# Tiles that TensorE streams, laid out with their even columns first and read in turns

## The chip, the cores and the metric

The kernel runs on one core of a Trainium2 chip. The metric is the device time of one execution, in microseconds (us). TensorE is called PE in the profile's rows (PEld is its weight load), VectorE DVE, ScalarE ACT, GpSimd POOL and SyncE SP.

## The reference

Two layers over a stream `x` of 1024 positions and 1024 channels, in float32. The first layer is a gated multi-scale causal pooling mixer, the second a gated sliding-window attention (window 128, 16 heads, 2 shared key/value heads) with sinks and a relative-position bias. Cut to what matters:

```
h = modulate(rmsnorm(x, norm_g[0]), shift, scale)          # layer 0
u, z = split(h @ a_w_in, 2)
p = trailing means of u over 2, 4, 8, 16 positions, minus u
y = (grouped(p @ a_w_group) * a_scale * silu(z)) @ a_w_out
x = x + gate * y
k, v = split(modulate(rmsnorm(x, kv_norm_g), ...) @ w_kv)  # shared by the heads
h = modulate(rmsnorm(x, norm_g[1]), shift, scale)          # layer 1
q, z = split(h @ b_w_in, 2)
per block of 128 queries, with this and the previous block of 128 keys:
    s = q k / 8 + pos_bias, masked to the band
    o = softmax(s with one sink per head) v
y = (o * silu(z)) @ b_w_out
x = x + gate * y
return rmsnorm(x, final_g)
```

## The kernel before, in words

Channels lie on the 128 partitions and positions along the free dimension, so that a tile of activations is 128 channels by 512 positions (`H = 512`, half of the sequence, index `q`). Every product of two float32 matrices is made from three matmuls: each operand is split into a high part (rounded to the 4-byte type fp32r) and a low part (what is left), and high times high, high times low and low times high are added up in one PSUM bank. The stationary operand is a 128x128 piece of a weight, the moving operand ("what TensorE streams") is the 128x512 tile of activations.

So each tile of activations is written twice. ScalarE writes the high part (`nc.scalar.copy` or `nc.scalar.activation` with an fp32r output), and VectorE the low part (a subtraction of the high part from the source). GpSimd does this in one place (`split_wg`). These pairs stand in `split_wg`, `first_h` and `first_l`, `pool_split`, `block_sums`, `split_g`, `Modulated.fold_h` and `fold_l`, `keys`, `attend` (the transposed probabilities `ph`, and the heads' outputs that go back into `qt`) and `Second.step`. The matmuls that stream these tiles are in `join_mm` (L308), `first_mm` (L375), `product` (L648), `passes` (L213), `dense_mm` (L200 to L202), `dense_step` (L1222 to L1224), `scores` in `attend` (L1358 and L1359, whose moving operands are the keys `KH` and `KL`) and `blend` (L1422 and L1423, which stream `ph` and its masked copy `pp`). Transposes (L1392, L1557), the sums of squares (L161, L1703), the spreading of a row (L173, L1720) and the last 128 positions' output product (L1580 to L1582, where the weights are the moving operand) stream other tiles.

The order on each engine is fixed when the program is built. Up to the keys and values it is the order of the code (on VectorE and ScalarE partly that of the tile framework). From there on (the attention, about 600 us into the span to its end) a small planner sets it: `note` records each step with its engine and an assumed length, `in_order` keeps TensorE's steps in the order in which they were recorded and places those of the other engines by these lengths. VectorE is where most of its choices fall: preparing the second half's activations (`xn`, then `hm`, in `Second.step`), the softmax rows, the splits and the residual adds share its queue.

Of the kernel before, what the change touches and what calls it, by code (L numbers as in the profile page):

```python
# [12 lines left out]
F32 = mybir.dt.float32  # L13
# [5 lines left out]
P = 128  # L19
# [36 lines left out]
SLOT_FILL = 32  # L56


@with_exitstack
def trunk(ctx, tc, xT, c, pack, ada_first, ada_rest, wu0_in, wg0_in, wa, wg, wao, wkv,  # L60
# [156 lines left out]
    with ExitStack() as sa:  # L217
# [74 lines left out]
        def split_wg(ci):  # L292
            nc.scalar.copy(out=wgs[0][:, ci, :], in_=wgr[:, ci, :])
            nc.gpsimd.tensor_sub(out=wgs[1][:, ci, :], in0=wgr[:, ci, :],
                                 in1=wgs[0][:, ci, :].bitcast(F32))
# [9 lines left out]
        def join_mm(m, ps, ci, passes=(0, 1, 2)):  # L305
            for s in passes:
                a, b = ((0, 0), (0, 1), (1, 0))[s]
                mm(ps, wus[ci][:, a, m * P:(m + 1) * P], wgs[b][:, ci, :],  # L308
                   start=ci == 0 and s == 0, stop=ci == 3 and s == 2)
# [42 lines left out]
        def first_h(k, q):  # L352
# [4 lines left out]
            nc.scalar.activation(h, first_f(k, q), AF.Identity, bias=b, scale=1.0)  # L357

        def first_l(k, q):
            _, b, h, l = first_parts(k, q)  # L360
            nc.vector.scalar_tensor_tensor(out=l, in0=first_f(k, q), scalar=b,
                                           in1=h.bitcast(F32), op0=ALU.add, op1=ALU.subtract)
# [3 lines left out]
        def first_mm(k, q, passes=(0, 1, 2)):  # L366
# [6 lines left out]
            for s, i in order:  # L373
                w, hl = ((0, 0), (1, 0), (0, 1))[s]
                mm(psu[i, q], w0[k // 2][:, k % 2, w, i * P:(i + 1) * P], block(k, q)[hl],  # L375
# [189 lines left out]
        def pool_split(g, ct, u):  # L565
            cur = pooled(g, u)
            p = pts[ct] = xp.tile([P, 2, T], F32R, tag="x", name="p", bufs=4)
            nc.scalar.copy(out=p[:, 0, :], in_=cur)
            nc.vector.tensor_sub(out=p[:, 1, :], in0=cur, in1=p[:, 0, :].bitcast(F32))
# [7 lines left out]
        def block_sums(j):  # L577
# [13 lines left out]
            for i, s, a, shift, b, op0, op1 in parts:  # L591
# [5 lines left out]
                nc.scalar.copy(out=sum_part(i, j, 0), in_=s)  # L597
            for i, s, *_ in parts:
                nc.vector.tensor_sub(out=sum_part(i, j, 1), in0=s,
                                     in1=sum_part(i, j, 0).bitcast(F32))  # L600
# [50 lines left out]
        def pair_products(ws, evac):  # L651

            b_acts = lambda q, c: lambda k, hl: block(4 * c + k, q)[hl]
            s_acts = lambda i: lambda k, hl: sum_part(i, k, hl)
# [49 lines left out]
        z_acts = lambda k, hl, q: block(k, q)[hl]  # L704
# [87 lines left out]
        def split_g(k, raws):  # L792
# [7 lines left out]
            for q in range(2):  # L800
                t = slot("gh") if q == 1 and k >= 14 else g_units[q][:, k % 2]
                g_parts[k, q] = t[:, 0, :], t[:, 1, :]
                nc.scalar.copy(out=t[:, 0, :], in_=raws[q])
                nc.vector.tensor_sub(out=t[:, 1, :], in0=raws[q], in1=t[:, 0, :].bitcast(F32))
# [19 lines left out]
        with tc.manual_schedule(engines={ET.PE}):  # L824
            nxt = w_first
            for i, (kind, g, j) in enumerate(steps):
# [19 lines left out]
                else:  # L846
                    for t in range(2):

                        ps = gemm_full(w, t * 512, lambda k, hl, q: pts[k][:, hl, half(q)],
# [11 lines left out]
            def g_acts(hf):  # L861
                return lambda k, hl, q: g_parts[8 * hf + k, q][hl]
# [84 lines left out]
        def last_chunk(i):  # L947

            n, c = late[i // 4], i % 4
            if c == 0:  # L950
                got[n] = bank(("S", "d")[i // 4 % 2])
            passes([(1, got[n])], ws[n, c // 2], (c % 2) * 512,
                   lambda k, hl, q: g_parts[4 * c + k, q][hl], 4, c == 0, c == 3)


        class Modulated:
# [6 lines left out]
            def fold_h(self, k, f):  # L963
# [7 lines left out]
                nc.scalar.activation(h, f, AF.Identity, bias=b, scale=1.0)  # L971

            def fold_l(self, k):
                _, b, h = self.args(k)
                nc.vector.scalar_tensor_tensor(
                    out=self.tiles[k // 2][:, k % 2, 1, :], in0=self.xn.pop(k), scalar=b,
                    in1=h.bitcast(F32), op0=ALU.add, op1=ALU.subtract)
# [5 lines left out]
            def __call__(self, k, i, q=0):  # L983
                return self.tiles[k // 2][:, k % 2, i, :]
# [231 lines left out]
    def dense_step(ps, w, off, acts, k, n, cols):  # L1216
# [8 lines left out]
        note(PE, {512: 0.69, 384: 0.53}[cols], f,  # L1225
# [9 lines left out]
    def keys(q, hk, ps=None):  # L1235
        def done(ps):
            cols = half(q)
            for kv in range(2):
                a, b = slice(kv * 64, kv * 64 + 64), slice((1 - kv) * 64, (1 - kv) * 64 + 64)

                def high(kv, a, to, h):
                    note(ACT, 0.55, lambda: nc.scalar.copy(out=KH[kv][to, cols], in_=ps()[a, :]),
                         [(ps, 0)], [(KHb[kv], (h, q))])

                def low(kv, a, to, h):
                    note(DVE, 0.63, lambda: nc.vector.tensor_sub(
                        out=KL[kv][to, cols], in0=ps()[a, :], in1=KH[kv][a, cols].bitcast(F32)),
# [84 lines left out]
    def attend(q, r, b):  # L1332
# [15 lines left out]
        def scores(j):  # L1348
# [6 lines left out]
            def f():  # L1355
                for e in range(2):
                    lhs = qt()[:, j, e, cols]
                    mm(s()[:, e, lo:], lhs, KH[kv][:, ks], start=True, stop=False)  # L1358
                    mm(s()[:, e, lo:], lhs, KL[kv][:, ks], start=False, stop=True)  # L1359
            note(PE, 0.48 if b else 0.46, f,  # L1360
# [28 lines left out]
        def turn():  # L1389
# [6 lines left out]
        note(ACT, 0.55, lambda: nc.scalar.copy(out=cur()[:, 0], in_=tp()), [(tp, 0)], [(cur, 0)])  # L1396
        note(DVE, 0.63, lambda: nc.vector.tensor_sub(  # L1397
            out=cur()[:, 1], in0=tp(), in1=cur()[:, 0].bitcast(F32)),
            [(tp, 0), (cur, 0)], [(cur, 1)])
        parts = [(b, cur)]  # L1400
        if b:
            prev = tile_of("pp", bp, [P, 2, H], F32R, 1)
            v8 = lambda t: t.rearrange("p x (a i) -> p (x a) i", i=P)
            note(POOL, 1.12, lambda: nc.gpsimd.affine_select(  # L1404
                out=v8(prev()), in_=v8(cur()).bitcast(F32), pattern=[[0, 8], [-1, P]], base=-1,
# [3 lines left out]
                out=v8(cur()), in_=v8(cur()).bitcast(F32), pattern=[[0, 8], [1, P]], base=0,  # L1409
# [9 lines left out]
        def blend(x, blk, ph):  # L1419
            def f():  # L1420
                v = VS[:, 2 * blk + kv].rearrange("p x c -> p (x c)")
                mm(o(), v, ph()[:, 0], start=x == 0, stop=False)  # L1422
                mm(o(), v, ph()[:, 1], start=False, stop=x == len(parts) - 1)  # L1423
            note(PE, 0.46, f, [(VSb, (blk // 4, 0)), (VSb, (blk // 4, 1)), (ph, 0)]
# [14 lines left out]
        for e in range(2):  # L1439
# [5 lines left out]
        note(ACT, 0.36, lambda: nc.scalar.copy(out=qt()[:, :, 0, cols], in_=ofv()),  # L1445
             [(of, 0), (of, 1)], o_on(0))
        note(DVE, 0.56, lambda: nc.vector.tensor_sub(
            out=qt()[:, :, 1, cols], in0=ofv(), in1=qt()[:, :, 0, cols].bitcast(F32)),
# [3 lines left out]
    def heads(q, part, cs):  # L1452

        def acts(k, i):
# [3 lines left out]
                       lambda t: t[:, k % 2, i, cols])  # L1458
# [321 lines left out]
    class Second:  # L1780
# [5 lines left out]
        def step(self, k):  # L1786
            if k % 2 == 0:
# [7 lines left out]
            note(ACT, 0.66, lambda: nc.scalar.activation(  # L1795
                t()[:, k % 2, 0, :], f(), AF.Identity, bias=b, scale=1.0),
                [(f, 0)], [(t, (k % 2, 0))])
            note(DVE, 0.7, lambda: nc.vector.scalar_tensor_tensor(
                out=t()[:, k % 2, 1, :], in0=f(), scalar=b,
                in1=t()[:, k % 2, 0, :].bitcast(F32), op0=ALU.add, op1=ALU.subtract),  # L1800
                [(f, 0), (t, (k % 2, 0))], [(t, (k % 2, 1))])

        def __call__(self, k, i):
            return Ref(self.tiles[k // 2], ((k % 2, i),), lambda t: t[:, k % 2, i, :])
# [161 lines left out]
```

## Time and profile before

| what | value |
|---|---|
| median of 3 runs | 964.12 us (963.63 to 964.23) |
| span of the profiled execution | 961.6 us |
| TensorE, matmul | 951.3 us (99%), 4468 matmuls |
| TensorE, weight load | 795.6 us (83%) |
| VectorE | 756.2 us (79%) |
| ScalarE | 425.4 us (44%) |
| GpSimd | 143.1 us (15%) |

For the profiled execution the page gives its span, from the first instruction to the last; no time of its own stands beside it. The span is 2.5 us under the median of the runs. Matmuls overlap one another in the records (one lasts about 390 ns and the next starts 227 ns after it), so that TensorE's busy share tells only that it hardly ever pauses; how fast it goes is read from the distance between starts.

### The profile page before, as it was taken

To read this page: it belongs to the slowest core of one execution; us is meant where nothing else is said; L and a number is where in the kernel's file an instruction comes from. 1 tells how busy PE (TensorE), PEld (TensorE's weight loads), DVE (VectorE), ACT (ScalarE), POOL (GpSimd) and SP (SyncE) were. 2 spreads that over 40 slices of the span, in tenths; PEclk is the share of its full clock that TensorE was granted. 3 is DMA by queue.
4 is the path that set the end of the run, shared out by engine and by line. 5 is a ranking of instruction groups with operands and counts; after the bars stand their busy time and mean duration, and the time that the engine had idled before them with its cause. 6 is when DMAs were issued, how large, how long until landed. Compare 5 with 4: busy or idle time off the path is not lost.

```text
span 961.6 us, 12687 instructions
## 1 busy us (share of the span) xinstructions
PE 951.3 (99%) x4468; PEld 795.6 (83%) x4468; DVE 756.2 (79%) x1414; ACT 425.4 (44%) x872; POOL 143.1 (15%) x229
## 2 busy tenths in 40 slices
PE   9999999999999999999999999999999999999997
PEld 6788888888888888888888888888888888888887
DVE  6999899687978699686765559499999757777785
ACT  6535454333533344551122234367665344455434
POOL 2000000000000000000022100232222334344521
PEclk9999999999999999999999999999999999999999
DMA  9553531254135411788887725835666453447022
GB/s 346 184 173 119 188 132 47 107 197 153 44 109 189 147 59 55 268 294 304 290 300 261 269 82 186 317 132 185 200 221 247 155 172 118 149 154 196 2 88 88
DMA packets 52081, 166.57 MB, mean 173 GB/s; under 512 B 6705, under 2 KB 7857, under 8 KB 51890
## 3 DMA queue, kind: packets, MB, share of 16 engines
q1 hardware_dynamic: 39346, 119.63, 36.0%
q0 software_dynamic: 12240, 44.57, 13.9%
q10 hardware_dynamic: 432, 1.57, 0.5%
q8 instruction: 35, 0.57, 0.2%
q14 instruction: 28, 0.23, 0.1%
HBM read 129.04 MB, written 36.70 MB: 172 GB/s over the span
## 4 chain that ended last, share of the span: by engine, by line
PE 93%; DVE 3%; DMA 1%; issue 1%; ACT 1%; POOL 0%; DVEq 0%; ACTq 0%
PE ps_d L648 13%; PE ps_d L213 12%; PE ps_d L1222 9%; PE ps_d L1223 9%; PE ps_d L1224 9%; PE ps_S L213 8%; PE ps_S L648 6%; PE ps_tp L213 4%; PE ps_tp L648 3%; PE ps_o L648 3%; PE ps_o L213 3%; PE ps_d L375 2%; PE ps_S L1359 1%; PE ps_S L1358 1%; PE ps_tp L1392 1%; PE ps_o L1423 1%
## 5 line engine op out<-in xcount | busy, mean ns | idle before, releaser
L213 PE MATMUL ps_d<-gh,wh 128*128 128x512 f32 x224 | 81.9, 389 | 0.0
L240 DVE CUSTOM_DVE_ANT_0 tmp<-tmp,cact,pk 128x1024 f32<-128x1024 f32 x48 | 60.6, 1282 | 25.6 <-DMA tmp<-ada_rest 25.5
L648 PE MATMUL ps_d<-hs,ws 128*128 128x512 f32 x312 | 74.9, 389 | 0.0
L1373 ACT ACTIVATE P<-P,nm 128x129 f32<-128x129 f32 x128 | 50.2, 394 | 45.5 <-DVE nm L1369 45.3
L1222 PE MATMUL ps_d<-hm,wh 128*128 128x512 f32 x176 | 69.5, 395 | 0.0
L1223 PE MATMUL ps_d<-hm,wh 128*128 128x512 f32 x176 | 68.7, 390 | 0.0
L648 PEld LDWEIGHTS ps_d<-hs,ws 128*128 128x128 f32 x312 | 58.6, 188 | 12.1
L1224 PE MATMUL ps_d<-hm,wl 128*128 128x512 f32 x176 | 68.6, 390 | 0.0
L213 PE MATMUL ps_S<-gh,wh 128*128 128x512 f32 x192 | 67.1, 390 | 0.0
L648 PE MATMUL ps_d<-ha,ws 128*128 128x512 f32 x252 | 60.5, 389 | 0.0
L618 ACT CAST ws<-tw 128x512 fp32r<-128x512 f32 x52 | 32.0, 620 | 59.2 <-DVE tw L623 18.0
L648 PEld LDWEIGHTS ps_d<-ha,ws 128*128 128x128 f32 x252 | 47.3, 188 | 9.8
L540 POOL MEMSET tmp<- 128x16 f32 x12 | 1.3, 111 | 327.0 <-DVE adac L240 122.2
L213 PEld LDWEIGHTS ps_d<-gh,wh 128*128 128x128 f32 x224 | 42.1, 188 | 8.8
L126 ACT CAST wh<-raw 128x1024 fp32r<-128x1024 f32 x24 | 25.2, 1052 | 53.9 <-PE ps_d L213 44.5
L548 DVE TENSOR_TENSOR tmp<-tmp 128x1039 f32<-128x1039 f32 (+3 forms) x36 | 44.4, 1234 | 1.0
L213 PE MATMUL ps_d<-gh,wl 128*128 128x512 f32 x112 | 43.6, 389 | 0.0
L213 PEld LDWEIGHTS ps_S<-gh,wh 128*128 128x128 f32 x192 | 35.9, 188 | 7.3
L1435 DVE SCALAR_TENSOR_TENSOR of<-ps_o,ol 64x256 f32<-64x256 f32 x64 | 26.6, 416 | 18.9 <-ACT ol L1429 18.2
L1404 POOL TENSOR_SCALAR_AFFINE_SELECT pp<-ph 128x1024 fp32r<-128x1024 f32 x28 | 30.7, 1095 | 57.6 <-DVE ph L1397 57.5
L1224 PEld LDWEIGHTS ps_d<-hm,wl 128*128 128x128 f32 x176 | 33.0, 188 | 7.1
L1222 PEld LDWEIGHTS ps_d<-hm,wh 128*128 128x128 f32 x176 | 33.1, 188 | 6.2
(354 smaller groups left out, 2628.3 us busy)
## 6 DMA issues: line engine op xcount, KB each, us to landing
tmp<-ada_rest SPq DMA_DIRECT2D x42, 512.0 KB, 4.7
raw<-wa SPq DMA_DIRECT2D x28, 512.0 KB, 3.3
raw<-wao SPq DMA_DIRECT2D x20, 512.0 KB, 4.9
raw<-kw POOLq DMA_DIRECT2D x20, 512.0 KB, 4.2
wh<-kw POOLq DMA_DIRECT2D x19, 512.0 KB, 3.5
wl<-kw POOLq DMA_DIRECT2D x19, 512.0 KB, 4.3
ad<-ada_first SPq DMA_DIRECT2D x16, 512.0 KB, 5.4
x<-xT SPq DMA_DIRECT2D x32, 256.0 KB, 5.8
```

The costliest lines, as they stand in the source:

```text
L126: nc.scalar.copy(out=wh, in_=raw)
L213: mm(p, lhs, acts(k, hl, q), start=start and k == ks[0] and s == 0, stop=stop and k == ks[-1] and s == 2)
L240: nc.vector.tensor_tensor_reduce(out=raw, in0=raw, in1=ca, scale=0.5, scalar=pk[:, bcol:bcol + 1], op0=ALU.mult, op1=ALU.add, accum_out=ad ...
L548: nc.vector.tensor_add(out=nx[:, 2 * s - 1:], in0=cur[:, 2 * s - 1:], in1=cur[:, s - 1:PAD + T - s])
L618: nc.scalar.copy(out=ws[i][:, 0, :], in_=src)
L648: mm(ps, lhs, acts(k, hl), start=start and k == 0 and s == 0, stop=k == 3 and s == 2, skip_group_check=True)
L1222: mm(p, lh, a[0](), start=k == 0, stop=False)
L1223: mm(p, lh, a[1](), start=False, stop=False)
L1224: mm(p, ll, a[0](), start=False, stop=k == n - 1)
L1373: note(ACT, 0.41, lambda: nc.scalar.activation(pt()[:, i, :P + 1], pt()[:, i, :P + 1], AF.Exp, bias=nm()[:, i:i + 1], scale=-1.0, accum_ou ...
L1404: note(POOL, 1.12, lambda: nc.gpsimd.affine_select(out=v8(prev()), in_=v8(cur()).bitcast(F32), pattern=[[0, 8], [-1, P]], base=-1, channel ...
L1435: note(DVE, 0.36, lambda: nc.vector.scalar_tensor_tensor(out=of()[e * 64:(e + 1) * 64, :], in0=o()[0:64, es], scalar=0.5, in1=ol()[0:64, e ...
```

## The change

The tiles named above are written with their even columns first and their odd columns behind them, and TensorE reads them with an access pattern that takes one column from the first half and one from the second in turns. The columns thus reach the array, and PSUM, in the order in which they did before. Two kinds of views do this; the second does it in each block of 128 columns, for tiles of which blocks are used alone:

```diff
+def lies(t):
+    return t.rearrange("p (b c) -> p b c", b=2)
+def apart(t):
+    return t.rearrange("p (c b) -> p b c", b=2)
+def moving(t):
+    return t.rearrange("p (b c) -> p c b", b=2)
+def lies_by_block(t):
+    return t.rearrange("p (a b c) -> p a b c", b=2, c=P // 2)
+def apart_by_block(t):
+    return t.rearrange("p (a c b) -> p a b c", b=2, c=P // 2)
+def moving_by_block(t):
+    return t.rearrange("p (a b c) -> p a c b", b=2, c=P // 2)
```

The instruction that makes a part reads its source with a step of two columns (`apart`) and writes two runs (`lies`); the matmul's moving operand is `moving(...)`. The weights (stationary operands) stay as they were. No instruction is added or removed. Typical places:

```diff
 def first_h(k, q):
-    nc.scalar.activation(h, first_f(k, q), AF.Identity, bias=b, scale=1.0)
+    nc.scalar.activation(lies(h), apart(first_f(k, q)), AF.Identity, bias=b, scale=1.0)
 def split_g(k, raws):
-    nc.scalar.copy(out=t[:, 0, :], in_=raws[q])
-    nc.vector.tensor_sub(out=t[:, 1, :], in0=raws[q], in1=t[:, 0, :].bitcast(F32))
+    raw, hi, lo = apart(raws[q]), lies(t[:, 0, :]), lies(t[:, 1, :])
+    nc.scalar.copy(out=hi, in_=raw)
+    nc.vector.tensor_sub(out=lo, in0=raw, in1=hi.bitcast(F32))
 def g_acts(hf):
-    return lambda k, hl, q: g_parts[8 * hf + k, q][hl]
+    return lambda k, hl, q: moving(g_parts[8 * hf + k, q][hl])
 scores (in attend)
-    mm(s()[:, e, lo:], lhs, KH[kv][:, ks], start=True, stop=False)
+    mm(s()[:, e, lo:], lhs, moving_by_block(KH[kv][:, ks]), start=True, stop=False)
 ph (in attend), read from PSUM
-    in0=tp(), in1=cur()[:, 0].bitcast(F32)
+    in0=apart_by_block(tp()), in1=lies_by_block(cur()[:, 0]).bitcast(F32)
 the mask of ph, on GpSimd
-    pattern=[[0, 8], [1, P]]
+    pattern=[[0, 8], [1, 2], [2, P // 2]]
 the heads' output, of -> qt: by halves of each block of 128, except in the last block
+    if q == 1 and r > 1 and c == 3:
+        ofs, oq = ofv, lambda i: qt()[:, :, i, cols]
```

In the last block of 128 positions those tiles are stationary operands, and lie as before. The planner's assumed lengths are changed too:

```diff
-        note(PE, {512: 0.69, 384: 0.53}[cols], f,
+        note(PE, {512: 0.65, 384: 0.49}[cols], f,
-            note(PE, 0.48 if b else 0.46, f,       # scores
+            note(PE, 0.45, f,
-            note(PE, 0.46, f, ...)                 # blend
+            note(PE, 0.435, f, ...)
-            note(ACT, 0.66, lambda: nc.scalar.activation(      # Second.step
+            note(ACT, 0.72, lambda: nc.scalar.activation(
```

With these the order on TensorE, GpSimd and SyncE stays what it was. On VectorE and ScalarE steps of the attention change places with neighbours. Two places on VectorE are shown; `hm` and `xn` prepare the second half's activations, `of` adds up a block's heads, `COPY_PREDICATED` and `ISA P,nm` are softmax rows, `ph` and `qt` are splits, `wl` is a split of a weight. The first stands about 645 us into the span. Before:

```order
L1798 SCALAR_TENSOR_TENSOR hm<-xn,adac,hm 128x512
L1792 SCALAR_TENSOR_TENSOR xn<-x,acol,rb_5052 128x512
L1798 SCALAR_TENSOR_TENSOR hm<-xn,adac,hm 128x512
L1362 COPY_PREDICATED ps_S<-tri,ps_S 128x2x128
L1397 TENSOR_TENSOR ph<-ps_tp,ph 128x512
L1362 COPY_PREDICATED ps_S<-tri,ps_S 128x2x128
L1369 ISA P,nm<-ps_S,bias,nsink 128x128
```

Now:

```order
L1840 SCALAR_TENSOR_TENSOR hm<-xn,adac,hm 128x512
L1471 SCALAR_TENSOR_TENSOR of<-ps_o,ol 64x256
L1395 COPY_PREDICATED ps_S<-tri,ps_S 128x2x128 x2
L1431 TENSOR_TENSOR ph<-ps_tp,ph 128x512
L1402 ISA P,nm<-ps_S,bias,nsink 128x128
```

One pair of preparation steps has moved behind the softmax rows, and half of a head sum ahead of them. The second place is about 728 us into the span, in the last blocks of the first half's attention. Before:

```order
L1353 MEMSET ps_S 128x2x128
L1798 SCALAR_TENSOR_TENSOR hm<-xn,adac,hm 128x512 x2
L1447 TENSOR_TENSOR qt<-of,qt 128x2x128
L1322 SCALAR_TENSOR_TENSOR szb<-szb,ps_d 128x512
L1681 TENSOR_TENSOR wl<-raw_5994,wh 128x1024
L1397 TENSOR_TENSOR ph<-ps_tp,ph 128x512
L1362 COPY_PREDICATED ps_S<-tri,ps_S 128x2x128 x2
L1435 SCALAR_TENSOR_TENSOR of<-ps_o,ol 64x256 x2
```

Now:

```order
L1386 MEMSET ps_S 128x2x128
L1355 SCALAR_TENSOR_TENSOR szb<-szb,ps_d 128x512
L1834 SCALAR_TENSOR_TENSOR xn<-x,acol,rb_5052 128x512
L1488 TENSOR_TENSOR qt<-of,qt 128x2x128
L1471 SCALAR_TENSOR_TENSOR of<-ps_o,ol 64x256 x2
L1431 TENSOR_TENSOR ph<-ps_tp,ph 128x512
L1395 COPY_PREDICATED ps_S<-tri,ps_S 128x2x128 x2
```

The two `hm` steps and the weight's split are placed later, and the head sums come ahead of the softmax rows.

92 lines of the change are left out of this document (52 added, 40 removed).

## The prediction

> **What bounds the kernel now.** The page first: busy time, the slices, and the heading of the chain.
>
> ```profile
> span 961.6 us, 12687 instructions
> PE 951.3 (99%) x4468; PEld 795.6 (83%) x4468; DVE 756.2 (79%) x1414; ACT 425.4 (44%) x872; POOL 143.1 (15%) x229
> PE   9999999999999999999999999999999999999997
> DVE  6999899687978699686765559499999757777785
> PEclk9999999999999999999999999999999999999999
> PE 93%; DVE 3%; DMA 1%; issue 1%; ACT 1%; POOL 0%; DVEq 0%; ACTq 0%
> ```
>
> TensorE is busy in every slice at the full granted clock, and 93% of the chain that ended last is TensorE. VectorE comes near to it in several slices (digit 9), so it is the second bound. A matmul's bar overlaps the next one's, so what one costs is the distance between starts. The timeline of TensorE gives that: start, length, line, operation, shape, count.
>
> ```profile
> 300.47 2.88 PE L648 MATMUL ps_o<-hs,ws 128*128 128x512 f32 x12
> 303.19 2.88 PE L648 MATMUL ps_d<-ha,ws 128*128 128x512 f32 x12
> ...
> 904.23 0.28 PE L1358 MATMUL ps_S<-KH,qt 128*128 128x256 f32 x1
> ...
> 905.18 0.40 PE L1222 MATMUL ps_d<-qt,wo 128*128 128x512 f32 x1
> ...
> 935.77 0.33 PE L1222 MATMUL ps_d<-qt,wo 128*128 128x384 f32 x1
> ...
> 946.52 0.34 PE L1224 MATMUL ps_d<-qt,wo 128*128 128x384 f32 x1
> 946.69 1.04 PE L1557 MATMUL ps_S<-ident,x 128*128 128x128 f32 x8
> 947.49 0.36 PE L1580 MATMUL ps_d<-wo,qt 128*128 128x256 f32 x1
> 947.69 0.28 PE L1581 MATMUL ps_d<-wo,qt 128*128 128x256 f32 x1
> 947.80 0.28 PE L1582 MATMUL ps_d<-wo,qt 128*128 128x256 f32 x1
> ```
>
> Twelve matmuls of 512 columns take 303.19 - 300.47 = 2.72 us, 226.7 ns each. From 935.77 to 946.52 lie 62 steps of 384 columns: 173.4 ns each. The 128 columns between them cost 53.3 ns, 0.4164 ns a column. At that rate 512 columns are 213.2 ns and 384 are 159.9 ns, so both sizes pay a further 13.5 ns that doesn't grow with the columns. The eight of 256 columns from 904.23 to 905.18 take 118.8 ns each, 12.2 ns over their 106.6 ns. The eight transposes and the matmul behind them take 947.69 - 946.69 = 1.00 us; less 0.12 us for that matmul (118.8 ns above), a transpose takes 110 ns: twice the column price of its 128 columns (106.6 ns) and 3.4 ns more. It loads a 128x128 piece as every other matmul does, so the 13.5 ns is no price of the weight load as such. Nor does the weight load set the pace:
>
> ```profile
> L648 PEld LDWEIGHTS ps_d<-hs,ws 128*128 128x128 f32 x312 | 58.6, 188 | 12.1
> ```
>
> Its 188 ns is longer than the 173.4 ns at which the 384-column matmuls run. By these rows the fixed 13.5 ns goes with the way in which fp32r tiles are streamed, and this is what the change touches.
>
> **The change part by part.** *Matmuls.* Of 4468, the other streams (their groups below, with L1581, L1582, L1720, L1703, L161, L436 and L1275 in the same view) are 128 + 24 + 22 + 48 + 54 + 16 + 4 + 8 + 8 = 312: transposes L1392, rows L173 and L1720, the last product, sums of squares, warming, the row L436, transposes L1275 and L1557. That leaves 4156 that change: 4 groups of 56 with 256 columns, 3 of 32 with 384, 32 with 128, and so 3804 with 512.
>
> ```profile
> L1392 PE MATMUL ps_tp<-ident,P 128*128 128x128 f32 x128 | 19.2, 272 | 0.6 <-DVE P L1382 0.6
> L1358 PE MATMUL ps_S<-KH,qt 128*128 128x256 f32 x56 | 14.6, 293 | 0.0
> L1224 PE MATMUL ps_d<-qt,wo 128*128 128x384 f32 x32 | 10.7, 335 | 0.0
> L1580 PE MATMUL ps_d<-wo,qt 128*128 128x256 f32 x16 | 4.8, 298 | 0.0
> L419 PE MATMUL ps_S<-ones 128*128 128x128 f32 x16 | 3.5, 406 | 1.0 <-DVE ones L103 1.0
> L173 PE MATMUL ps_tp<-ident,rs 128*128 128x128 f32 x24 | 3.2, 274 | 0.0
> ```
>
> No row streams columns in turns from two halves, so the new price is bounded. The lower end is the bare column rate, 213.2 ns. The upper end of a gain is the transposes' remainder, 216.6 ns; no gain at all, and a loss, are rivals below. I take the middle, 214.9 ns, 11.8 ns less than now: the column rate is the same at two sizes, so only the fixed part can go, and a stream without it (the transposes) keeps little. Saved: 3804 x 11.8 = 44.9 us, 96 x 11.8 = 1.1 us, 224 x (12.2 - 1.7) = 2.4 us; the 32 small ones at nothing. Together 48.4 us (41.1 with 216.6 ns; 55.4 with 213.2 ns).
>
> The Trainium skill ("TensorE: Matmul & The Clock Gate", Back-to-back issue gap) gives N/2.4 + 2.5 ns for an isolated warm matmul, 215.8 ns at 512 columns. The trace's 226.7 ns differs from it by 10.9 ns and decides what is paid now; a fall to the page's figure would save, by an estimate from it, 3804 x 10.9 = 41.5 us on the 512-column matmuls, inside the bounds above.
>
> *What doesn't follow TensorE.* Windows of 24 us show busy time by engine, PE first, DVE third:
>
> ```profile
> 0.00:24.00 24.00, 21.89 (x88) 16.42 (x89) 16.27 (x25) 15.23 (x24) 7.12 (x26) 1.00 0.95 346
> 24.00:48.00 24.00, 23.25 (x121) 19.16 (x120) 23.09 (x40) 12.77 (x24) 2.04 (x2) 1.00 0.51 183
> 48.00:72.00 24.00, 24.00 (x108) 19.87 (x107) 23.87 (x40) 9.46 (x16) 0.00 (x0) 1.00 0.52 175
> 72.00:96.00 24.00, 24.00 (x108) 19.87 (x106) 23.46 (x33) 13.82 (x27) 0.00 (x0) 1.00 0.34 117
> 240.00:264.00 24.00, 24.00 (x108) 19.87 (x107) 23.59 (x33) 13.12 (x21) 0.33 (x3) 1.00 0.14 44
> 336.00:360.00 24.00, 24.00 (x107) 19.88 (x107) 23.90 (x31) 10.92 (x17) 0.22 (x2) 1.00 0.18 64
> 360.00:384.00 24.00, 24.00 (x108) 19.88 (x107) 22.94 (x32) 10.10 (x16) 0.11 (x1) 1.00 0.14 45
> 648.00:672.00 24.00, 24.00 (x119) 20.16 (x118) 23.60 (x66) 16.72 (x44) 5.77 (x8) 1.00 0.50 175
> 672.00:696.00 24.00, 24.00 (x126) 20.35 (x126) 23.50 (x55) 15.80 (x36) 5.79 (x7) 1.00 0.58 190
> 696.00:720.00 24.00, 24.00 (x120) 20.18 (x119) 23.60 (x61) 15.44 (x41) 5.03 (x6) 1.00 0.66 230
> 720.00:744.00 24.00, 24.00 (x124) 20.36 (x123) 23.58 (x65) 14.56 (x40) 6.64 (x9) 1.00 0.66 242
> 744.00:768.00 24.00, 24.00 (x121) 20.19 (x120) 17.78 (x48) 9.26 (x27) 8.10 (x13) 1.00 0.52 172
> ```
>
> The first two stretches wait for loads and splits, not for TensorE: I take back the whole gain of their 209 matmuls, 209 x 11.8 = 2.5 us. A full stretch of 24 us holds about 106 long matmuls and shrinks by 1.25 us to 22.75. Where VectorE is busy for longer than that, it can set the pace: 648 to 744 by 94.28 - 91.0 = 3.3 us, 336 to 384 by 1.3, 48 to 96 by 1.8, 240 to 264 by 0.8: 7.2 us. Some of it is made good next door (744 to 768 has 17.78), so I take 6 us, with 0 and 12 as its ends.
>
> *The writers of the tiles.* ScalarE writes the high parts at 44% busy, under TensorE and ahead of VectorE; at nothing. If ScalarE became slower, VectorE's low parts, which wait for it, would be late next. GpSimd's mask reads as many elements in the same order in memory and only counts columns otherwise: nothing, covered by its 85% of idle time; without that, `blend` would wait for `pp`. VectorE's low parts read every second column and write two runs. The rows nearest to that:
>
> ```profile
> L1280 DVE TENSOR_TENSOR VS<-ps_d,VS 128x512 fp32r<-128x512 f32 x2 | 1.4, 691 | 0.1
> L1246 DVE TENSOR_TENSOR KL<-ps_d,KH 64x512 fp32r<-64x512 f32 x8 | 5.5, 687 | 5.3 <-ACT KH L1242 5.3
> L1397 DVE TENSOR_TENSOR ph<-ps_tp,ph 128x512 fp32r<-128x512 f32 x32 | 21.9, 685 | 10.1 <-ACT ph L1396 9.9
> L1798 DVE SCALAR_TENSOR_TENSOR hm<-xn,adac,hm 128x512 fp32r<-128x512 f32 x16 | 12.0, 767 | 0.0
> L294 POOL TENSOR_TENSOR wgs<-wgr,wgs 128x512 fp32r<-128x512 f32 x4 | 5.9, 1472 | 11.2 <-ACT wgs L293 11.2
> ```
>
> `VS` is written in runs of 64 columns with gaps, `KL` in one run, at 691 and 687 ns: runs cost nothing. No row has a step of two, so its price lies between nothing and, at worst, a second pass over the elements (a doubling, as for the transposes' columns). I take nothing, as for the runs. The same holds for GpSimd's four low parts of the group weights (`wgs`, last row), which TensorE waits for in its first 24 us: nothing, at worst twice 1.472 us each, 6 us.
>
> *The order.* TensorE's is the same. In the stretch 648 to 744 VectorE's `xn` and `hm` go behind softmax rows and splits, and residual adds have two or three other steps ahead. The first waits behind softmax rows that TensorE's transposes need sooner; the second has four PSUM banks as cover, some 10 us at twelve matmuls a bank (4 x 2.72). If that cover were gone, a late `hm` would stop the second half's queries. Taken at nothing, inside the 0 to 12.
>
> Sum: 48.4 - 2.5 - 6 = 39.9 us off the profiled span of 961.6, to 921.7; with the 2.5 us between span and median, 964.1 - 39.9 = 924 us. Its own range: at best 55.4 and no loss, 909; at worst 41.1 - 2.5 - 12 - 6 = 20.6, 944.
>
> **The rivals.**
>
> *VectorE pays for the step of two (can end slower).* The low parts on VectorE are 176 tiles of 512 columns: 16 first activations, 24 of the pools, 16 sums, 32 gated tiles, 32 modulated (`hm`), 8 keys, 32 `ph`, and 32 halves for `qt`. At the 685 ns of `ph` they are 121 us. By estimate from the code's order, 44 of them fall in 624 to 768 (16 `hm`, 16 `ph`, 4 keys, 16 halves), 34 in 48 to 168, and 8 in 336 to 384: 86 x 0.685 = 59 us where VectorE is busy nearly all the time and TensorE, once faster, has no slack. Doubled, the step costs 59 us beside the 6 taken: 983, slower; at 25% dearer, 939. It decides the sign from 40 / 59 = 68%. Against it: the `VS` row.
>
> *The fixed 13.5 ns stays.* It may belong to starting any fp32r matmul, whatever the pattern. The last product speaks for it: it streams two separate runs of 128 columns, and its 947.80 - 947.69 = 0.11 us, to the hundredth that the rows give, is about the 118.8 ns of one run of 256. Then only the reordering on VectorE is left: 962 to 966.
>
> *Streaming in turns is slower.* Each column then comes from elsewhere than the last, 512 fetches instead of a run. If a column then costs what it costs in a transpose (twice 0.4164 ns), a 512-column matmul takes 426 ns, 200 more than now: 3804 x 0.2 = 761 us, about 1725 us. It decides from 13.5 / 512 = 0.026 ns a column. Against it: one jump, in the last product, costs nothing that the rows show; but it is one, not 511.
> The Trainium skill ("Advanced Engine Details and Errata", SBUF Cachelines) has this rule: a 16-byte line needs at least two hits in a row, and a new line on each access pays. By it this rival holds; no run here shows it.
>
> **How the numbers follow.** Forecast 0.72; VectorE dearer 0.10 (0.08 of it still faster, mostly 930 to 958, 0.01 within the bound, 0.01 slower); the fixed price stays 0.06 (0.05 within the bound, 0.01 faster by the reordering); slower streaming 0.12. The likeliest gives 924 us. The range 908 to 958 takes in the forecast's own and most of VectorE's, 0.8 together, and leaves out the last two. A measurement of this kernel tells 0.2% (2 us) from no change. Faster by more than that: 0.72 + 0.08 + 0.01 = 0.81; within it 0.01 + 0.05 = 0.06; slower 0.01 + 0.12 = 0.13.
>
> **What would show it.** Twelve matmuls of 512 columns in 2.56 to 2.60 us instead of 2.72, and 384 columns in 160 to 164 ns, say that the fixed part went; 2.72 or more says that it did not. `ph` and `hm` on VectorE near 685 and 767 ns say that the step of two is free. TensorE's idle time, or matmuls far apart, in 48 to 96 and about 620 to 710 us would be VectorE's part; over 12 us of it would prove my 6 too small.

## The result: 10 us faster, where 40 were forecast

The changed kernel takes 953.89 us (median of 5 runs, 952.19 to 959.44) beside 964.12 us: a ratio of 0.991, 95% interval 0.9886 to 0.9935. The interval lies below 1, so it is faster, as forecast, but by a quarter of the 40 us. Here and below a median is that of the fast runs: one of four runs with the step on VectorE (1612.38 us, granted clock 0.557) and one of five with the order restored from PSUM (977.0 us, 0.924) fell in a slower state and are left out. The profile after, first the page (busy time and the heading of the chain):

```profile
span 951.3 us, 12686 instructions
PE 916.2 (96%) x4468; PEld 796.9 (84%) x4468; DVE 775.9 (82%) x1414; ACT 456.6 (48%) x872; POOL 151.0 (16%) x229
PE 51%; DVE 30%; DMA 8%; issue 6%; ACT 5%; SPq 0%; DVEq 0%; ACTq 0%; POOLq 0%; POOL 0%
```

TensorE is busy for 35.1 us less, but it now pauses: span less busy time was 961.6 - 951.3 = 10.3 us and is 951.3 - 916.2 = 35.1 us. Of the chain that ended last it holds 51% instead of 93%; VectorE holds 30%. VectorE and ScalarE have become busier by 19.7 and 31.2 us, with the same number of instructions. The timeline of TensorE gives the matmuls' price, as before the change by the distance between starts:

```profile
301.12 2.75 PE L678 MATMUL ps_o<-hs,ws 128*128 128x512 f32 x12
303.70 2.75 PE L678 MATMUL ps_d<-ha,ws 128*128 128x512 f32 x12
306.30 0.38 PE L240 MATMUL ps_S<-p,wh 128*128 128x512 f32 x1
...
896.32 0.27 PE L1391 MATMUL ps_S<-KH,qt 128*128 128x256 f32 x1
...
897.10 0.28 PE L1392 MATMUL ps_S<-KL,qt 128*128 128x256 f32 x1
...
924.75 0.33 PE L1253 MATMUL ps_d<-qt,wo 128*128 128x384 f32 x1
...
936.28 0.33 PE L1255 MATMUL ps_d<-qt,wo 128*128 128x384 f32 x1
```

Twenty-four matmuls of 512 columns take 5.18 us, 215.8 ns each (226.7 before). Seven steps of 256 columns take 0.78 us, 111.4 ns (118.8 before), and 71 steps of 384 take 11.53 us, 162.4 ns (173.4 before). So the fixed part of the price fell from 13.5 to 2.6 ns at 512 columns, at the column rate of before.

Who makes TensorE wait now? The view of waits (total us, times, longest), its first rows. Then windows of 24 us: the second of the execution, for its granted clock (0.93), and the four with the largest pauses behind the first 24 us (in these four TensorE was busy for the whole 24 us before the change):

```profile
PE ps_o L240 <- DVE wl L155: 4.4, 2, 2.4
PE ps_S L1391 <- DVE ps_S L1386: 2.5, 2, 1.8
PE ps_tp L240 <- DVE wl L155: 2.1, 2, 1.1
PE ps_d L1255 <- DMA raw<-kw: 1.9, 1, 1.9
```

```profile
24.00:48.00 24.00, 22.47 (x114) 19.17 (x114) 21.95 (x36) 13.69 (x24) 2.04 (x2) 0.93 0.48 177
96.00:120.00 24.00, 21.09 (x93) 16.91 (x92) 23.16 (x35) 13.56 (x26) 0.00 (x0) 1.00 0.44 151
360.00:384.00 24.00, 21.34 (x96) 17.73 (x96) 23.49 (x32) 9.75 (x15) 0.11 (x1) 1.00 0.12 40
456.00:480.00 24.00, 21.25 (x96) 17.98 (x96) 17.70 (x27) 4.55 (x6) 0.00 (x0) 1.00 0.82 284
480.00:504.00 24.00, 20.39 (x93) 17.57 (x94) 16.37 (x24) 3.98 (x5) 2.92 (x5) 1.00 0.87 305
```

No single wait is large. In 96 to 120 and 360 to 384 VectorE is busy for 23.2 and 23.5 us of 24, and TensorE waits for what ScalarE and VectorE write. The largest pauses lie in 456 to 504, 6.4 us. There VectorE is busy for only 16 to 18 us of 24, and TensorE waits for its low part of a weight (`wl`, 6.5 us in four waits), which is read without a step; VectorE itself waits 13.7 us for loads between 452 and 504, and the DMA engines are busy for 0.82 and 0.87 of the time. The reason why VectorE and ScalarE are busier stands in their groups (the number behind the busy time is the mean ns of one). First before the change, then after:

```profile
L803 ACT CAST gh<-gr 128x512 fp32r<-128x512 f32 x18 | 10.8, 619 | 6.0 <-DMA gr<-kept_g 5.9
L804 DVE TENSOR_TENSOR gh<-gr,gh 128x512 fp32r<-128x512 f32 x18 | 11.8, 684 | 0.7 <-ACT gh L803 0.7
```

```profile
L834 ACT CAST gh<-gr 128x512 fp32r<-128x512 f32 x18 | 15.6, 925 | 6.6 <-DMA gr<-kept_g 6.6
L835 DVE TENSOR_TENSOR gh<-gr,gh 128x512 fp32r<-128x512 f32 x18 | 14.5, 834 | 3.6 <-ACT gh L834 3.6
L1840 DVE SCALAR_TENSOR_TENSOR hm<-xn,adac,hm 128x512 fp32r<-128x512 f32 x16 | 14.6, 926 | 0.0
L1431 DVE TENSOR_TENSOR ph<-ps_tp,ph 128x512 fp32r<-128x512 f32 x32 | 21.9, 685 | 8.5 <-ACT ph L1429 8.3
```

These writers, which now read SBUF with a step of two, are 49% dearer on ScalarE and 22% dearer on VectorE (`hm` on VectorE 926 ns instead of 767). The other tiles of 512 columns or more that are read from SBUF so are 27 to 46% dearer on ScalarE and 17 to 23% on VectorE. `ph`, which reads PSUM with a step of two, stays at 685 ns. The prediction had read this step's price off the runs of `VS` and of `KL`, and had put ScalarE's at nothing.

So the theory is that the writers' step of two took the gain. Its rivals: the changed order on VectorE and ScalarE did, or VectorE and the loads had no slack for a faster TensorE, whatever the writers cost.

### The profile page after: what moved, and what is told of

Read it like the earlier page. It is cut to its first block, busy times and chain, and to the rows that moved or that the text cites. A ratio compares the mean times of both kernels' runs of the same rounds, so it can differ in the third digit from the quotient of the medians.

```text
span 951.3 us, 12686 instructions
## 1 busy us (share of the span) xinstructions
PE 916.2 (96%) x4468; PEld 796.9 (84%) x4468; DVE 775.9 (82%) x1414; ACT 456.6 (48%) x872; POOL 151.0 (16%) x229
## 4 chain that ended last, share of the span: by engine, by line
PE 51%; DVE 30%; DMA 8%; issue 6%; ACT 5%; SPq 0%; DVEq 0%; ACTq 0%; POOLq 0%; POOL 0%
PE ps_d L1255 7%; PE ps_d L1253 7%; PE ps_d L1254 7%; PE ps_d L678 5%; PE ps_d L240 5%; PE ps_S L240 4%; DMA tmp<-ada_rest 3%; DVE tmp L576 3%; PE ps_S L678 2%; DVE ws L649 2%; PE ps_tp L240 2%; DVE ad L267 2%; PE ps_tp L678 2%; DVE wl L155 1%; DVE tw L653 1%
## 5 line engine op out<-in xcount | busy, mean ns | idle before, releaser
L240 PE MATMUL ps_d<-gh,wh 128*128 128x512 f32 x224 | 79.7, 379 | 0.0
L678 PE MATMUL ps_d<-hs,ws 128*128 128x512 f32 x312 | 72.1, 380 | 1.4 <-ACT ws L648 1.0
L1253 PE MATMUL ps_d<-hm,wh 128*128 128x512 f32 x176 | 67.4, 383 | 0.0
L1254 PE MATMUL ps_d<-hm,wh 128*128 128x512 f32 x176 | 66.7, 379 | 0.0
L240 PE MATMUL ps_S<-gh,wh 128*128 128x512 f32 x192 | 65.1, 380 | 0.0
L678 PE MATMUL ps_d<-ha,ws 128*128 128x512 f32 x252 | 57.8, 379 | 0.0
L1439 POOL TENSOR_SCALAR_AFFINE_SELECT pp<-ph 128x1024 fp32r<-128x1024 f32 x28 | 32.9, 1176 | 60.5 <-DVE ph L1431 60.4
L240 PE MATMUL ps_d<-p,wh 128*128 128x512 f32 x96 | 36.6, 381 | 2.4 <-ACT p L598 1.7
L1255 PE MATMUL ps_d<-hm,raw 128*128 128x512 f32 x96 | 36.5, 380 | 1.9 <-DMA raw<-kw 1.9
L678 PE MATMUL ps_S<-hs,ws 128*128 128x512 f32 x156 | 36.3, 381 | 1.5 <-ACT ws L648 1.5
```

Of the source, the lines that this page charges most:

```text
L240: mm(p, lhs, acts(k, hl, q), start=start and k == ks[0] and s == 0, stop=stop and k == ks[-1] and s == 2)
L678: mm(ps, lhs, acts(k, hl), start=start and k == 0 and s == 0, stop=k == 3 and s == 2, skip_group_check=True)
L1253: mm(p, lh, a[0](), start=k == 0, stop=False)
L1254: mm(p, lh, a[1](), start=False, stop=False)
L1255: mm(p, ll, a[0](), start=False, stop=k == n - 1)
L1439: note(POOL, 1.12, lambda: nc.gpsimd.affine_select(out=v8(prev()), in_=v8(cur()).bitcast(F32), pattern=[[0, 8], [-1, 2], [-2, P // 2]], ba ...
```

## The experiments

### One half of the change at a time

**Reading in turns alone.** Every writer reads and writes in plain runs; the sums then come out in another order of columns.

```diff
 def apart(t):
-    return t.rearrange("p (c b) -> p b c", b=2)
+    return t.rearrange("p (b c) -> p b c", b=2)      # the same in the form by blocks, p and of
```

> The matmuls stream in turns as in the changed kernel, but the writers read and write their tiles plainly (columns in their natural order), so the sums come out in another order of columns; only the price of the step of two in the writers is left out. Theory W (the writers' step of two ate the gain: ScalarE 619 to about 930 ns, VectorE 684 to about 830 ns): matmuls at 215.8 ns, writers back at 619 and 684 ns, time 926 to 936 us. Rival S (VectorE was full anyway and sets the pace as soon as TensorE is faster): 946 to 954 us although the writers are cheap again.

Measured: 934.89 us (933.24 to 936.73), ratio 0.9703 (0.9687 to 0.972). Page and groups:

```profile
span 933.5 us, 12686 instructions
PE 913.4 (98%) x4468; PEld 799.8 (86%) x4468; DVE 757.9 (81%) x1414; ACT 424.3 (45%) x872; POOL 149.1 (16%) x229
L834 ACT CAST gh<-gr 128x512 fp32r<-128x512 f32 x18 | 10.7, 616 | 7.7 <-DMA gr<-kept_g 7.6
L835 DVE TENSOR_TENSOR gh<-gr,gh 128x512 fp32r<-128x512 f32 x18 | 11.9, 686 | 2.0 <-ACT gh L834 2.0
```

These writers cost what they did before, TensorE's pauses fall from 35.1 to 20.1 us (in 456 to 504 from 6.4 to 1.6), and 19 us come back. The writers are the larger part of the loss, though not all of it.

**Writing apart alone.** TensorE reads in plain runs (`moving` returns its tile as it is); the writers are those of the changed kernel.

> The other half alone: writers read every second column and lay the tiles apart, matmuls read the tiles plainly (the sums are of columns in another order). Theory W: matmuls back at 226.7 ns, writers at 930 and 830 ns; under the slower TensorE most of their extra 50 us is hidden, 964 to 974 us. Rival S: the writers' extra is harmless, 963 to 965 us.

Measured: 964.21 us (963.17 to 965.91), ratio 1.0008 (0.9998 to 1.0017). The groups:

```profile
L834 ACT CAST gh<-gr 128x512 fp32r<-128x512 f32 x18 | 11.5, 665 | 5.7 <-DMA gr<-kept_g 5.7
L835 DVE TENSOR_TENSOR gh<-gr,gh 128x512 fp32r<-128x512 f32 x18 | 11.9, 686 | 0.4 <-ACT gh L834 0.4
```

The step of two costs VectorE nothing and ScalarE 7% where TensorE streams plainly. So "the step of two is dear" is refuted as a price of the instruction; it is dear beside a TensorE that reads in turns from two halves. The prediction's price of nothing was right for the instruction alone and wrong beside the other half of the change.

**Writing in turns instead of reading with a step.** The writers read in runs and write their columns to the two halves in turns, so that the tiles lie as in the changed kernel.

```diff
-    lies:  "p (b c) -> p b c"      apart: "p (c b) -> p b c"
+    lies:  "p (b c) -> p c b"      apart: "p (c b) -> p c b"
```

> The same tiles and the same streams as in the changed kernel, with the loops of the writers turned round: the source is read in its natural order, the parts are written in turns to the two halves (and VectorE reads the high part in turns). Theory W in its narrow form (the price is that of reading SBUF with a step of two): writers near 619 and 684 ns, 926 to 940 us. If any pattern with jumps costs the writers: 0.9 us and more per tile, 950 us or slower. Rival S: 946 to 954 us whatever they cost.

Measured: 1002.88 us (999.69 to 1007.36), ratio 1.0412 (1.038 to 1.0443).

```profile
L1429 ACT CAST ph<-ps_tp 128x512 fp32r<-128x512 f32 x32 | 34.6, 1081 | 11.9 <-PE ps_tp L1425 5.9 <-POOL P L1374 5.5
L1431 DVE TENSOR_TENSOR ph<-ps_tp,ph 128x512 fp32r<-128x512 f32 x32 | 35.6, 1112 | 15.0 <-ACT ph L1429 14.9
```

A write in turns is dearer still, on both engines and from PSUM too: `ph` takes 1081 and 1112 ns instead of 585 and 685, and theory W falls in its narrow form. On VectorE the instruction also reads the high part in turns, and TensorE streams in turns as in the changed kernel, so that this is no price of the write by itself. This is no way out.

**The old order.** The changed kernel, planned with the assumed lengths of the kernel before.

> The changed kernel with the planner's lengths of before, so that VectorE and ScalarE take their steps in the attention in the order of before. Theory W and rival S: no great matter, 950 to 957 us. Rival O (the new order in the attention lost the gain): 940 us or less, with TensorE's waits between 600 and 760 us gone.

Measured: 956.59 us (955.47 to 959.85), ratio 0.9933 (0.9913 to 0.9954). VectorE's and ScalarE's changed places are not the loss; the medians lie 2.7 us apart, the new order ahead, and the intervals overlap.

### Which engine's reads, and beside which stream

To reading in turns alone, the step of two is added on most of one engine's SBUF sources, and on none of the other's.

```diff
-    nc.scalar.copy(out=hi, in_=raw)              # and its like
+    nc.scalar.copy(out=hi, in_=stepped(raws[q])) # stepped: "p (c b) -> p b c"
```

> The reading-in-turns kernel (934.9 us), in which ScalarE alone reads its SBUF sources with a step of two and VectorE reads them in runs; the high parts thus belong to other columns than the low ones. Theory C1 (each reader with a step of two is slowed by TensorE's stream in turns, by itself): ScalarE's gh 890 to 930 ns, hm 970 to 990, VectorE's gh 686 and hm 745 as before; since ScalarE is 45% busy and VectorE's low parts wait for it, half of the 19 us: 940 to 947 us. Rival C2 (the dear thing is that ScalarE and VectorE read with a step of two at the same time): gh on ScalarE under 720 ns, 934 to 938 us.

> The reading-in-turns kernel, in which VectorE alone reads its SBUF sources with a step of two and ScalarE reads them in runs; the low parts thus belong to other columns than the high ones. Theory C1: VectorE's gh about 830 ns and hm 890 to 925, ScalarE's gh 617 and hm 721 as before; 937 to 945 us. Rival C2: VectorE's gh under 710 ns and hm under 770, 934 to 938 us.

Measured: with the step on ScalarE 941.12 us (940.22 to 943.52), ratio 0.9774 (0.976 to 0.9789); with the step on VectorE 942.57 us (941.75 to 944.31), ratio 0.9787 (0.9772 to 0.9802). `gh` in the first, then in the second:

```profile
L838 ACT CAST gh<-gr 128x512 fp32r<-128x512 f32 x18 | 15.0, 875 | 6.2 <-DMA gr<-kept_g 6.2
L839 DVE TENSOR_TENSOR gh<-gr,gh 128x512 fp32r<-128x512 f32 x18 | 12.0, 688 | 2.5 <-ACT gh L838 2.2
```

```profile
L838 ACT CAST gh<-gr 128x512 fp32r<-128x512 f32 x18 | 10.8, 618 | 8.4 <-DMA gr<-kept_g 8.2
L839 DVE TENSOR_TENSOR gh<-gr,gh 128x512 fp32r<-128x512 f32 x18 | 14.3, 830 | 2.5 <-ACT gh L838 2.5
```

Each engine is slowed by itself (C1 holds, though ScalarE's 875 ns is a little under its 890, and C2 falls); 6.2 and 7.7 us, together 13.9 of the 19. ScalarE's share is nearly as large as VectorE's although it is busy for 48% only: its high part stands ahead of VectorE's low part, and both ahead of the matmul. The other 5 us are the two together, or the places that these runs left plain (`wgs`, `p`, and `of` to `qt`); no run separates them.

The Trainium skill ("SBUF — State Buffer", Who interferes with whom) has contention only in the port pair that VectorE and GpSimd share, and gives TensorE and ScalarE read ports of their own. The trace doesn't agree: from writing apart alone to the changed kernel ScalarE's read goes from 665 to 925 ns with nothing but TensorE's read pattern changed.

What of TensorE's stream is it? The changed kernel again, with all its writers; TensorE takes the columns in turns from neighbouring groups of four (16 bytes apart) instead of from two halves (256 columns, 1 KB apart). The sums come out in another order.

```diff
 def moving(t):
-    return t.rearrange("p (b c) -> p c b", b=2)
+    return t.rearrange("p (a b c) -> p a c b", b=2, c=4)
```

> The changed kernel, with all its writers, in which TensorE takes the columns of the tiles in turns from neighbouring groups of four (as in the neighbouring-lines kernel, 215.8 ns for 512 columns) instead of from two halves; keys, heads and probabilities as in the changed kernel. The sums come out in another order of columns. Theory T (what makes the readers with a step of two dear is TensorE's reading in turns from two places far apart): ScalarE's gh and hm fall back to about 665 and 767 ns and VectorE's to 686 and 745, as where TensorE streams plainly; 935 to 941 us. Rival R (it is the faster stream as such, from wherever it comes): gh 890 to 930 ns and hm 970 to 990 on ScalarE, 830 and 890 to 925 on VectorE; 950 to 958 us.

Measured: 935.52 us (932.43 to 937.11), ratio 0.9699 (0.9674 to 0.9724).

```profile
span 934.3 us, 12686 instructions
PE 914.7 (98%) x4468; PEld 801.6 (86%) x4468; DVE 760.0 (81%) x1414; ACT 431.4 (46%) x872; POOL 148.4 (16%) x229
L834 ACT CAST gh<-gr 128x512 fp32r<-128x512 f32 x18 | 11.5, 659 | 8.2 <-DMA gr<-kept_g 8.0
L835 DVE TENSOR_TENSOR gh<-gr,gh 128x512 fp32r<-128x512 f32 x18 | 12.0, 687 | 3.9 <-ACT gh L834 3.8
```

This is as fast as reading in turns alone, and `gh` is back at 659 and 687 ns, with each writer's step of two in place and the matmuls at 215.8 ns. So the loss needs both: a writer's step of two, and a stream whose successive columns come from two places 1 KB apart. Theory T holds for the streams that were changed. In the attention keys, heads and probabilities still come in turns from places 64 columns (256 bytes) apart. The `hm` of that stage takes 809 ns on ScalarE and 851 on VectorE there, against 766 and 802 in writing apart alone and 975 and 926 in the changed kernel. That these streams slow it in part fits, but no run separates it, and the distance at which the cost sets in wasn't looked for.

### What the stream itself costs

Four probes change only the order in which TensorE takes the columns, on reading in turns alone. The sums come out in other orders.

> The reading-in-turns kernel, in which TensorE takes the even columns of a run first and then the odd ones (a step of two, 8 bytes) instead of columns from two halves in turns; the sums come out in another order of columns. Theory A (fp32r tiles read in one run pay the fixed 11 ns because neighbouring columns come one right behind the other; any order without neighbours avoids it): 512 columns every 215.8 ns, about 935 us. Rival B (only two streams far apart, read in turns, avoid it): 226.7 ns, 962 to 966 us. Rival L (a step costs bandwidth in SBUF): over 230 ns a matmul, over 975 us.

> The reading-in-turns kernel, in which TensorE takes columns in turns from two neighbouring groups of four (0, 4, 1, 5, 2, 6, 3, 7, 8, 12 ...) instead of from two halves; the sums come out in another order of columns. Known: from two halves 512 columns every 215.8 ns; even columns and then odd ones 451 ns. Theory H (what doubles the price is a column whose neighbour is not taken while it is still at hand; two places are at hand at a time): neighbours follow each other at a distance of two, as in the halves, so 215.8 ns and about 935 us. Rival N (any small step between columns that follow each other is dear; the distance of 1 KB between the halves is what helps): 400 ns or more, 1700 us or more.

> The reading-in-turns kernel, in which TensorE takes two neighbouring columns from the first half, then two from the second, and so on (0, 1, 256, 257, 2, 3 ...); keys and heads, which are used by blocks, stay with one column in turns; the sums come out in another order. Theory A (the fixed 11 ns goes with neighbours that follow each other at once): 512 columns every 226.7 ns or a few ns under it, 955 to 966 us. Rival B (it goes with reading one long run; any change between two runs avoids it): 215.8 ns, about 935 us. By theory H it can't be much dearer than 226.7 ns, since every column's neighbour follows it at once.

> The reading-in-turns kernel, in which TensorE takes columns in turns from four quarters (0, 128, 256, 384, 1 ...) instead of two halves; the sums come out in another order. If more than two places are at hand at a time: 215.8 ns for 512 columns and about 935 us. If only two are: every column is fetched by itself, as with even and then odd columns, 451 ns and about 1850 us.

The timeline of TensorE in each, in this order: a group of twelve matmuls and the group behind it, whose start ends the twelve:

```profile
304.36 5.59 PE L678 MATMUL ps_d<-hs,ws 128*128 128x512 f32 x12
309.78 2.44 PE L678 MATMUL ps_o<-hs,ws 128*128 128x512 f32 x5
```

```profile
149.98 2.75 PE L678 MATMUL ps_d<-hs,ws 128*128 128x512 f32 x12
152.57 2.75 PE L678 MATMUL ps_tp<-hs,ws 128*128 128x512 f32 x12
```

```profile
152.00 4.12 PE L678 MATMUL ps_d<-ha,ws 128*128 128x512 f32 x12
155.94 4.12 PE L678 MATMUL ps_d<-hs,ws 128*128 128x512 f32 x12
```

```profile
300.82 3.56 PE L678 MATMUL ps_d<-ha,ws 128*128 128x512 f32 x12
304.22 3.56 PE L678 MATMUL ps_d<-hs,ws 128*128 128x512 f32 x12
```

| columns taken | 512 columns | time |
|---|---|---|
| one run (before) | 226.7 ns | 964 us |
| in turns, two halves | 215.8 ns | 934.9 us |
| in turns, neighbouring groups of four | 215.8 ns (2.59 us for twelve) | 931.7 us, one run |
| in turns, four quarters | 283 ns (3.40 us) | 1175.2 us, one run |
| pairs in turns, two halves | 328 ns (3.94 us) | 1304.4 us, one run |
| even, then odd | 452 ns (5.42 us) | 1852.7 us, one run |

The first probe refutes theory A (any order without neighbours avoids the 11 ns) and bears out its rival L, with a price that nobody had named. The second agrees with theory H, and the third refutes it, since it had the pairs near 226.7 ns: two neighbours that follow each other at once, and then a jump, are dearer than a jump at every column. For the four quarters neither forecast holds. What rule makes these six prices stays open. The rival of slower streaming had the right size for a stream like the first probe (about 1850 us against the 1725 worked out), so that the prediction's 0.12 for it was about a real cliff, one access pattern away.

The Trainium skill ("Advanced Engine Details and Errata", SBUF Cachelines) asks for two hits on each 16-byte line and has a new line on every access pay. Neither half agrees here: even-then-odd takes two columns in a row from each line and doubles the price, and two halves in turns change the line at every column and lower it.

### A version without strided reads in SBUF, and what is left

The tiles lie in natural order and TensorE reads them in turns, so that the columns of the first half come to stand on the even places of PSUM and those of the second on the odd ones; the instructions that read PSUM anyway (copies, splits, residual adds) take every second column there and restore the order. The scores and the last block are streamed as before the change.

```diff
-    nc.scalar.copy(out=dst, in_=ps)
+    nc.scalar.copy(out=lies(dst), in_=apart(ps))
-    return lambda k, hl, q: g_parts[8 * hf + k, q][hl]
+    return lambda k, hl, q: moving(g_parts[8 * hf + k, q][hl])
```

> Tiles lie with their columns in natural order, TensorE streams them in turns (so the sums stand in PSUM with even and odd columns apart in position), and the instructions that read PSUM anyway take every second column there, so that everything behind them is in natural order again. No tile in SBUF is read with a step of two. The scores, the masked tiles' last block and the weights are streamed as before the change. Theory C (a step of two costs much only where it reads SBUF while TensorE streams in turns; from PSUM it is free, as ph at 585 and 685 ns in the changed kernel): hm 721 and 745 ns, gh about 620 and 686 ns, KL and the readers of PSUM within 3% of before; 934.9 us of the reading-in-turns kernel plus 1.5 us for the plain scores, 933 to 939 us. Rival (a step of two costs from PSUM too once nearly every evacuation has it): the evacuations 15% or more dearer, residual adds and keys late, 945 us or more.

Measured: 937.90 us (935.55 to 942.88), ratio 0.9742 (0.9716 to 0.9768).

```profile
span 934.8 us, 12694 instructions
PE 914.5 (98%) x4468; PEld 800.0 (86%) x4468; DVE 756.2 (81%) x1414; ACT 424.4 (45%) x872; POOL 144.7 (15%) x229
```

VectorE's busy time is the 756.2 us of the kernel before, and ScalarE's 424.4 is within 1 us of its 425.4: a step of two out of PSUM costs nothing that shows, and the rival falls. The median lies within the 933 to 939 expected. This version leaves out nothing of the reference and is faster than both kernels: 25 us under the one before, 16 under the changed one.

Last, what of the remaining pauses is VectorE's: the same kernel with VectorE's modulation products cut to an eighth of their columns, which leaves out most of their sums.

> The order-in-PSUM kernel (939.3 us median, profiled span 934.8), in which VectorE's 58 modulation products, 128x1024 and 1.28 us each, take only 128 of their 1024 columns; this leaves out most of the sums behind the modulation. All loads stay, TensorE's and GpSimd's order too; on VectorE and ScalarE a few steps change places. VectorE is lighter by about 1 us a product, most of it between 0 and 420 us. Theory S (what is left of the loss against the sum of TensorE's savings comes from VectorE, which has no slack in 72 to 144 and at 360 us): the 5.9 us of pauses between 72 and 144 and at 360 go down to under 1.5, span 928 to 931. Rival D (they come from loads and from the order): pauses stay at 4 us or more, span 933 to 936.

Measured: 930.24 us (928.67 to 932.48), ratio 0.9652 (0.9631 to 0.9673). The windows, first with the full products and then with the light ones:

```profile
96.00:120.00 24.00, 22.61 (x102) 18.61 (x101) 20.66 (x32) 11.27 (x21) 0.11 (x1) 1.00 0.53 189
360.00:384.00 24.00, 23.01 (x106) 19.52 (x105) 19.74 (x30) 10.73 (x18) 0.00 (x0) 1.00 0.44 151
456.00:480.00 24.00, 22.46 (x105) 19.35 (x104) 17.25 (x27) 4.16 (x6) 2.39 (x4) 1.00 0.91 298
```

```profile
96.00:120.00 24.00, 23.61 (x109) 20.04 (x108) 21.01 (x34) 11.52 (x23) 0.11 (x1) 1.00 0.51 172
360.00:384.00 24.00, 23.00 (x106) 19.52 (x105) 19.55 (x31) 12.39 (x22) 0.00 (x0) 1.00 0.56 197
456.00:480.00 24.00, 24.00 (x113) 21.02 (x112) 10.72 (x23) 5.04 (x6) 3.19 (x6) 1.00 0.91 333
```

The span falls by 5.0 us (934.8 to 929.8), the median by 7.7, for 58 us less of VectorE. At 96 us the pause falls from 1.4 to 0.4 us, at 456 from 1.5 to nothing, and at 360 it stays at 1.0. Over 72 to 144 and 360 to 384 together the pauses fall from 3.9 us (the expectation had put them at 5.9) to 2.6, between what theory S (under 1.5) and rival D (4 or more) had; the span of 929.8 is in theory S's range. So theory S is right in part: VectorE accounts for some of what is left; the rest, loads or order, wasn't separated.

## Why the prediction was wrong in size

It had the sign and the place of TensorE's gain right: twelve matmuls of 512 columns in 2.59 us and 384 columns in 162.4 ns, as it had named. The 953.9 us lies inside its range of 908 to 958, but outside the forecast's own 909 to 944. What brought it there is only in part the rival that widened the range, so that this hit is in part luck. Its sum went wrong like this, each span less its TensorE busy time:

| kernel | span | TensorE busy | pauses |
|---|---|---|---|
| before | 961.6 | 951.3 | 10.3 |
| changed | 951.3 | 916.2 | 35.1 |
| reading in turns alone | 933.5 | 913.4 | 20.1 |
| step on ScalarE, on VectorE | 939.2, 942.6 | 913.4, 915.3 | 25.8, 27.3 |
| neighbours and all writers | 934.3 | 914.7 | 19.6 |
| order restored from PSUM | 934.8 | 914.5 | 20.3 |

- **The step that failed: the writers at nothing.** "ScalarE writes the high parts at 44% busy, under TensorE and ahead of VectorE; at nothing", and for VectorE "I take nothing, as for the runs". Measured: 17.8 us of span (951.3 against 933.5), 19.0 of the medians. The rows were used rightly for the instruction alone (writing apart alone costs 0.9 us beside its own runs of before, ratio 1.0008), but they showed these writers beside a TensorE that streams runs, and the change alters that stream too. The cost is one of the combination, which no row of before could show; a range for it had been kept for VectorE (a rival, 25% dearer at 939) and none for ScalarE, whose share is 6.2 us.
- **TensorE's term, 48.4 us, was 44.2.** 3804 x 10.9 = 41.5, 96 x 11.0 = 1.1, 224 x 7.4 = 1.7. The forecast's 11.8 ns lay between the bounds; the upper bound for the new price, 216.6 ns, was nearest to the 215.8 measured. (By its own parts that bound saves 38.4 + 1.0 + 2.0 = 41.4 us, not 41.1, which changes nothing here.) The Trainium skill ("TensorE: Matmul & The Clock Gate", Back-to-back issue gap) gives 215.8 ns for 512 columns: the trace after agrees at 512 columns, the one before does not.
- **VectorE's slack and the first 48 us, 8.5 us together.** With plain writers the pauses grew by 9.8 us, near the 8.5. But a late start shorter than what a matmul's bar overlaps the next (0.38 - 0.22 = 0.16 us) shows as no pause: TensorE's busy time fell by 37.9 us there and not by 44.2, and the missing 6.3 are late or slow starts too, 16.1 in all. So the 6 was too small even without the writers. In 24 to 48 us 114 matmuls start instead of 121, where I had expected no gain and no loss; the granted clock is 0.93 there, in reading in turns alone 0.86. In both TensorE waits 0.82 us at 30 us (0.43 before the change), and then the clock falls; in reading in turns alone it is 0.50 from 32 to 38 us, and the twelve matmuls of 512 columns there take 5.26 us instead of 2.85 before. That is 2.4 of the 6.3 us. The sum had no term for it, and no run separates what sets it off.
- **The order, at nothing:** right (956.6 us with the old one, 953.9 with the new).
- **GpSimd, at nothing:** its four `wgs` rose from 1472 to 1873 ns each, 1.6 us together; TensorE's pauses in the first 24 us went from 2.1 to 2.3 us.
- **The rivals.** VectorE did pay, about 22% on its SBUF reads, close to the 25% that the rival priced at 939; alone this cost 7.7 us, and ScalarE's reads, which the rival didn't have, cost 6.2. The fixed 13.5 ns fell to 2.6. Streaming in turns was not slower.

From the span of 921.7 forecast to 951.3: 4.2 (TensorE's term) + 7.6 (late starts beyond 8.5) + 17.8 (writers beside the new stream) = 29.6 us.

## What to carry to other kernels

When a change alters how one engine reads a memory and also how others read it, price the pair and not each alone: a row from before prices an instruction beside the old neighbour. Where the order of columns must be mended, mend it where PSUM is read, since a step of two was free there and cost 22% (VectorE) and 49% (ScalarE) on `gh` in SBUF beside this stream. And before changing a streaming pattern, probe its variants one by one: orders that look alike ranged from 216 to 452 ns.

## What the hardware showed that was not expected

- A stream in one run pays 11 ns more per matmul than one in turns (226.7 and 215.8 ns at 512 columns, 173.4 and 162.4 at 384).
- ScalarE's and VectorE's reads of SBUF with a step of two are free or about 7% dearer beside plain streams and beside turns 16 bytes apart (`gh` 659 to 665 and 686 to 687 ns), and 49% and 22% dearer beside turns 1 KB apart (925 and 834).
- Writing in turns to two halves, measured only beside a TensorE that reads in turns from two halves, costs 0.4 to 0.5 us for 512 columns on either engine, from PSUM too (585 to 1081 ns, 685 to 1112; on VectorE with the high part read in turns as well).
- Pairs in turns (328 ns) are dearer than single columns in turns (215.8 ns), and a step of two in TensorE's stream doubles its price.
